# Hybrid decoder step on one core: four moves in a hand-written instruction order

## The chip, the cores and the metric

The kernel runs on one core of a Trainium2 chip. The metric is the device time of one execution in microseconds (us); the figure for a kernel is the median of its runs. A separate execution was recorded by the hardware profiler, and every time of a single instruction below comes from that one. The engines are PE (matrix multiply; PEld is its weight load, which has rows of its own), DVE (vector), ACT (scalar), POOL (GpSimd) and SP, which here only issues transfers. Each engine works through its own instructions in order, and engines wait for each other through semaphores.

## What is computed

One layer of a decoder trunk, for a prompt of 512 tokens and for 8 samples of 4 tokens, 544 columns together, model width 1024, in float32:

```python
h = RMSNorm_pre(x)
x_r, q, k, v, g = split(h @ W_in)
A = RG_LRU(conv4(x_r))                        # 8 gate blocks
B = windowed_attention(q, k, v)               # 8 heads, window 128
m = (sigmoid(g_A) * (A @ W_A) + sigmoid(g_B) * (B @ W_B)) @ W_out
x = x + RMSNorm_post(m)
u = conv3(RMSNorm_pre2(x) @ W_up)             # 2 x 4096 columns
y = x + RMSNorm_post2((gelu(u_gate) * u_val) @ W_down)
```

Beside y the kernel returns new states. Two of them matter here: the last two up-projected rows of the prompt and of each sample (`p_ffn_conv`, `s_ffn_conv`), called the state rows below.

## The kernel before

**Products.** Every float32 operand is split in two parts, high and low, and each product is three passes on PE: high by high, high by low, low by high. ACT makes the high part of a weight tile (L283, L1463) and DVE the low part by a subtraction (L290, L168, called from `wsplit_lo` and `do_low`); in the first column POOL makes it. The names in the profile carry this: `wh_`/`wl_` are the parts of a weight, `hH`/`hL`, `b11H`, `fH`/`fL` those of an activation. The 544 columns go in two halves, 256 and 288 or 272 and 272.

**Order.** The order on PE is written out by hand throughout, and on ACT and DVE in all the code that the change touches: an instruction waits behind everything that was issued earlier on its engine, whether it needs it or not. The order on POOL and SP is left to the scheduler. In the mixer a `step` is one weight column for one half, followed by a `tick`; `start_at(t, gen)` puts a generator on a list, and `sides` runs its next piece when `now` has reached its time. In the feed-forward part a `slot` follows each product: it runs what `later` and `result` have put down for this turn, then `consumed` (which splits the weights four units ahead and issues loads ten units ahead), then `round_`, a tick of 0.5.

**The start (L480 to L499).** The first two blocks of 128 tokens are turned on PE (`turn_a`, tile `ps_ta`), ACT makes `hH` (L452) and DVE `hL` (L453, in the profile L177, the helper `stt`). The first weight column comes in two transfers, one for each four k; DVE casts its high parts (L285) and POOL subtracts. The products go to `pm_first`. Then follow `pmin` products of the next columns. `xsquare` sums squares for the norm.

**Gates (L1092 to L1118).** `gate_later` is a sigmoid on ACT over 544 columns. For a column of `gl` it runs one tick after the column is done, or, where `raw` holds, at tick `SCANS[7] + c - 1`, after the square roots of the scans. Exponential, sigmoid and square root need different function tables on ACT (ACT_TABLE_LOAD). The product that needs `gl` is `lo_done` (L1131).

**Norm beside the first up tiles (L1233, L1752 to L1758).** After W_out the second half's `norm_chain` (statistics `pst_m`, factors `rep_m`, residual `x`, squares `accx`, statistics `pst_f`, factors `rep_f`, normalised `h2t`, operands `b12`, `b22`) runs in pieces, one for each slot, beside sixteen products of the first half with eight early up columns (tile `pq`, weights `wl_e`, units 1 to 16). Its piece was put down in `round_`, after the split of that slot's weight unit.

**The end (L1765 to L1945).** The plan ends with down products `pmdn` of group 6 (weights `wh_dn`), then comes the last group, QL = 7, for the second half: eight products c0 to c7 with `wh_dl`/`wl_dl`. Their results are added by DVE to `ft` (L174), squared by ACT (`sq_ft`, L1182), and added up by DVE (`acc`). Three PSUM tiles serve `pmdn` in turn, so the third product after one needs that one's `ft` addition. Three products held back (columns 5 to 7 of group 6, first half) follow, with the statistics `pst_o` between them, then the factors `rep_o`, the token-major products `ptok`, `pend`, and the output. `x1_again` brings the residual back (DMAs on SP) and turns it (`px`, `xtok`); `ffn_states` (L1733) does, twice: eight transposes into two PSUM tiles (`pfs`, `pfp`), two copies on ACT into tiles `ffn_rows_s` and `ffn_rows_p` (L1743, L1744), two DMAs on POOL's queue (L1745, L1746). These tiles, `xtok`, `x1r`, `ft`, the parts of f and of the last weights come from one pool of 53 buffers (S, L143).

Of the kernel before, what the change touches and what calls it, by code (L numbers as in the profile page):

```python
# [19 lines left out]
KD = D // P  # L20
# [58 lines left out]
GATES = (51, 53, 55, 57, 72, 73, 74, 75)  # L79
# [44 lines left out]
def hawk_step(ctx, tc, I, O):  # L124
    nc = tc.nc
    act, dve, pool, pe = nc.scalar, nc.vector, nc.gpsimd, nc.tensor
# [16 lines left out]
    def S(name, dt=F32):  # L143
        return sp.tile([P, SLOT], dt, tag="s", name=name)
# [16 lines left out]
    def f32(ap):  # L161
        return ap.bitcast(F32)

    def mm(out, l, r, start, stop):
        pe.matmul(out, l, r, start=start, stop=stop)  # L165
# [10 lines left out]
    def stt(out, a, s_, b, op0, op1):  # L176
        dve.scalar_tensor_tensor(out=out, in0=a, scalar=s_, in1=b, op0=op0, op1=op1)  # L177
# [3 lines left out]
    side, now, serial, late, last, mids, after, taps = [], [0], [0], [], [], [], [], []  # L181

    def start_at(t, gen):
        serial[0] += 1
        side.append([t, serial[0], gen])
# [62 lines left out]
    def wname(i):  # L248
        return "_".join(str(z) for z in order[i])
# [11 lines left out]
    def wclaim(target):  # L261

        target = min(target, 2 * len(order))
        for i in range(len(wraw), min(len(order), (target + 1) // 2 + 2)):
            if target:
                wload(i)
        got = list(range(wnext[0], target))
        wnext[0] = max(wnext[0], target)
        return got

    def wsplit_hi(un, eng=None):
        i, u = un // 2, un % 2
        hl = []
        for x in "hl":
            if order[i] in in_slots:
                t_ = S(f"w{x}{u}_{wname(i)}", F32R)[:, 0:512]
                t_ = t_.rearrange("p (k n) -> p k n", k=4)
            else:
                t_ = wp.tile([P, 4, P], F32R, tag="w", name=f"w{x}{u}_{wname(i)}")
            hl.append(t_)  # L280
        raw = wraw[i][:, 4 * u:4 * u + 4, :]
        if eng is None:
            act.activation(hl[0], raw, AF.Copy)  # L283
        else:
            eng.tensor_copy(hl[0], raw)  # L285
        wunits[un] = hl
        return raw, hl

    def wsplit_lo(raw, hl, eng=None):
        (eng or dve).tensor_tensor(out=hl[1], in0=raw, in1=f32(hl[0]), op=ALU.subtract)  # L290
# [53 lines left out]
    def step(key, X, a, done, target=None, look=2, quick=False):  # L344

        first_ = key == order[0] and a == 0
        ps = first_ps if first_ else PM("pm" + "_".join(str(z) for z in key) + f"_{a}")
        if first_:
            pass
        elif quick:  # L350
            mmhalf(ps, key, X, a, range(4))
            now[0] += 0.5
            sides()
            mmhalf(ps, key, X, a, range(4, 8))
            done(a, ps)
        elif len(wunits) <= 2 * FIRST and a == 0 and key in order[1:FIRST]:
            mmhalf_low_last(ps, key, X, a)
        else:
            mmhalf(ps, key, X, a)
        tick(upto(key, a, look) if target is None else target, 0.5 if quick else 1)  # L360
        if first_:
            after.append(lambda: mids.insert(1, lambda: done(a, ps)))
        elif not quick:
            (last if len(wunits) <= 2 * FIRST and a == 0 else late).append(lambda: done(a, ps))
# [39 lines left out]
    def dummy(z):  # L404
        mm(pw[:, (z % 4) * P:(z % 4 + 1) * P], ones, ones, True, True)
# [23 lines left out]
    def xsquare(i, z, on_act):  # L429
        n = TOK[i][1]  # L430
        j_, x_, o_ = T(f"jk{i}_{z}")[:n, 0:512], xt[i, z][:n, 0:512], ss[:n, z, i:i + 1]
        if on_act:
            act.activation(j_, x_, AF.Square, accum_out=o_)
        else:
            dve.scalar_tensor_tensor(out=j_, in0=x_, scalar=1.0, in1=x_, op0=ALU.mult, op1=ALU.mult, accum_out=o_)
# [14 lines left out]
    def hsplit(k, a, ps):  # L450
        g = pv[:, G_PRE + k:G_PRE + k + 1]
        act.activation(h.get(k, a, 0), ps, AF.Copy, scale=g)  # L452
        stt(h.get(k, a, 1), ps, g, f32(h.get(k, a, 0)), ALU.mult, ALU.subtract)  # L453
# [4 lines left out]
    u0, u1 = wclaim(2)  # L458
    first_ps = PM("pm_first")

    def first_mm(k, i0, i1, start=False, stop=False):
        mm(first_ps[:, :256], wunits[k // 4][i0][:, k % 4, :], h.get(k, 0, i1), start, stop)
# [3 lines left out]
    def turn_a(z):  # L466
        for k in range(4 * z, 4 * z + 4):
            if not z:
                ps_ta.append(PX(f"ps_ta{k}"))
            for q in range(2):  # L470
                pe.transpose(turned_a(k)[:, q * P:(q + 1) * P], xtile(q, k), ident)

    def turned_a(k):
        return ps_ta[k % 4][:, k // 4 * 256:k // 4 * 256 + 256]

    def first_low(z):
        for k in range(4 * z, 4 * z + 4):
            first_mm(k, 1, 0, stop=k == KD - 1)

    turn_a(0)  # L480
    for z in range(FILL):
        dummy(z)
    for k in range(KD):
        if k % 4 == 0:
            raw, hl = wsplit_hi((u0, u1)[k // 4], eng=dve)
        hsplit(k, 0, turned_a(k))
        if k % 4 == 0:
            wsplit_lo(raw, hl, eng=pool)
        first_mm(k, 0, 0, start=k == 0)
        if k == 3:  # L490
            turn_a(1)
        if k % 4:
            first_mm(k - 1, 0, 1)
        if k % 4 == 3:
            first_mm(k, 0, 1)
        if k == 3:
            first_low(0)
    first_low(1)
    xsquare(1, 1, False)  # L499

# [539 lines left out]
    def once(f, *args):  # L1040
        f(*args)
        yield
# [39 lines left out]
    def gate_done(dst, c, name, raw):  # L1082
        def f(a, ps):
            lo, hi = HALF[a]
            if a == 0:
                dst[c] = S(f"{name}{c}")
            scaled(dst[c][:, lo:hi], ps, a)
            if a == 1 and not raw:
                start_at(now[0] + 1, once(gate_later, dst, c))
        return f  # L1090
# [19 lines left out]
        for a in range(2):  # L1110
            step(("ao", c), A, a, ao_done(c), look=1 if now[0] + 1 <= GATES[3] + 2 else 2)
    for c in range(8):
        raw = 75 + 2 * c > GATES[7] + 2 and c < 7
        for a in range(2):
            step(("in", 20 + c), h, a, gate_done(gl, c, "gl", raw), look=1 if now[0] + 1 <= GATES[7] + 2 else 2)
        if raw:
            start_at(SCANS[7] + c - 1, once(gate_later, gl, c))
# [267 lines left out]
    nearly = len(units)  # L1385
# [105 lines left out]
    def consumed(k=1, lag=1, limit=10 ** 6):  # L1491
        at[0] += k
        ahead(min(at[0] + AHEAD + more[0], limit), lag)
# [24 lines left out]
    def round_(dt=0.5):  # L1518
        tick(0, dt)
# [67 lines left out]
    def result(f, *args):  # L1587
        todo.setdefault(turn[0] + 1, []).insert(0, lambda: f(*args))

    def slot(k=1, lag=1, limit=10 ** 6):  # L1590

        for f in todo.pop(turn[0], []):
            f()
        if k:
            consumed(k, lag, limit)
        turn[0] += 1
        round_()


    ec, qps = {}, {}  # L1600
# [132 lines left out]
    def ffn_states():  # L1733
        os_ = O["s_ffn_conv"].rearrange("o b i (m n) -> (o b i m) n", n=D)
        op = O["p_ffn_conv"].rearrange("o b i (m n) -> (o b i m) n", n=D)
        for kk in range(2):
            px = PX(f"pfs{kk}")
            py = PX(f"pfp{kk}")
            for j in range(4):
                pe.transpose(px[:, j * P:(j + 1) * P], sfT[:, 4 * kk + j].rearrange("p r m -> p (r m)"), ident)  # L1740
                pe.transpose(py[:16, j * P:(j + 1) * P], stage_p[:, 4 * kk + j].rearrange("p r m -> p (r m)"), ident)
            o1, o2 = S(f"ffn_rows_s{kk}"), S(f"ffn_rows_p{kk}")
            act.copy(o1[:, 0:512], px)  # L1743
            act.copy(o2[:16, 0:512], py[:16, :])  # L1744
            pool.dma_start(out=os_[:, kk * 512:(kk + 1) * 512], in_=o1[:, 0:512])  # L1745
            pool.dma_start(out=op[:, kk * 512:(kk + 1) * 512], in_=o2[:16, 0:512])  # L1746
            yield
# [4 lines left out]
    for z in range(0, len(early), 2):  # L1752
        for u in range(2):
            for j in early[z:z + 2]:
                plain("e", j, u, 0)
                slot(1, 0, nearly)
        if z == 6:
            ffn_prev()  # L1758
    at[0], s_ = nearly - AHEAD, 0
# [5 lines left out]
    for i, x in enumerate(plan):  # L1765
        more[0] = min(4, max(0, i - len(plan) + LASTS))
        if x[0] == "s":
            pair(*x[1:])
            slot()
        elif x[0] == "q":  # L1770
            plain(*x)
            slot(x[3])
        else:
            _, q, c, a = x
            down(q, c, a, down_done(q, c))
            slot(a)
        if i == len(plan) - 8:
            start_at(now[0] + 1, x1_again())
            start_at(now[0] + 5, ffn_states())

    yp, ys = O["y_p"][0], O["y_s"].rearrange("b t d -> (b t) d")
    sq7 = {}
# [194 lines left out]
```

## Time and profile before

| what | value |
|---|---|
| median of 3 runs | 997.41 us (997.02 to 998.38) |
| profiled execution, its own time | 998.21 us |
| its span, first to last instruction | 996.4 us |
| mean granted PE clock | 0.997 |
| instructions | 20123 |
| busy: ACT, POOL | 561.3 us (56%), 160.6 us (16%) |
| transfers | 135.62 MB, mean 136 GB/s |

Times in the profile run from the start of the span; 1.8 us of the execution's own time lie outside it. A group row gives line, engine, operation, output and inputs, count and busy time; a bracket gives the idle time of the engine just before and what ended it. A matmul's end is modelled and overlaps the next one's start, so gaps of PE are read from start to start or from the weight loads.

### The profile page before, as it was taken

The page shows a single profiled execution, that of the slowest core. Times are in us where ns is not written, and L with a number is a line of the kernel's source. Part 1 is how long each engine was busy: PE and PEld are TensorE (multiplying, and loading weights), DVE is VectorE, ACT ScalarE, POOL GpSimd, SP SyncE. Part 2 cuts the span into 40 slices and gives each one's busy share as a digit, 9 for nine tenths or more (in the row PEclk, how much of TensorE's full clock was granted, in tenths as well). Part 3 has the DMA queues.
Part 4 walks back from the last instruction along what each step waited for, and adds up shares of the span by engine and source line. Part 5 has one row for each costly group of instructions (what it writes and reads, how often), then busy time and mean ns, then how long its engine had stood idle before and what let it go on. Part 6 is the DMA issues. An engine that isn't in the chain of part 4 may idle for free.

```text
span 996.4 us, 20123 instructions
## 1 busy us (share of the span) xinstructions
PE 984.2 (99%) x7783; PEld 973.6 (98%) x7783; DVE 745.8 (75%) x1609; ACT 561.3 (56%) x1358; POOL 160.6 (16%) x269
## 2 busy tenths in 40 slices
PE   9999999999999999999999999999999999999997
PEld 8999999999999999999999999999999999999986
DVE  6777678766848655688877778888888888888745
ACT  6544434468367525456767665656565656565642
POOL 2062000002505341210011111111111111111004
PEclk9999999999999999999999999999999999999999
DMA  7765222333323535246058585858585858577412
GB/s 207 190 219 183 66 84 86 107 86 100 91 65 105 176 112 151 63 135 180 15 130 182 134 189 131 189 130 189 129 190 129 191 127 191 128 185 197 148 46 90
DMA packets 210999, 135.62 MB, mean 136 GB/s; under 512 B 8845, under 2 KB 197021, under 8 KB 210872
## 3 DMA queue, kind: packets, MB, share of 16 engines
q1 hardware_dynamic: 198920, 112.72, 39.9%
q0 software_dynamic: 11920, 19.59, 11.9%
q10 hardware_dynamic: 64, 2.04, 0.6%
q8 instruction: 61, 1.00, 0.4%
q14 instruction: 34, 0.28, 0.1%
HBM read 111.78 MB, written 11.37 MB: 124 GB/s over the span
## 4 chain that ended last, share of the span: by engine, by line
PE 93%; issue 4%; DVE 2%; DMA 1%; ACT 0%; POOL 0%; SPq 0%; DVEq 0%; ACTq 0%; POOLq 0%
PE pmin L165 22%; PE pmdn L165 16%; PE pux L1526 15%; PE puy L1526 8%; PE pq L1526 6%; PE pmout L165 5%; PE pmao L165 5%; PE pmlo L165 5%; PE puz L1526 4%; PE pg L165 1%; PE psc L165 1%; PE pvp L165 1%; PE ptok L165 1%; PE pt L819 1%; DMA raw_in<-in_w_in_dram 0%
## 5 line engine op out<-in xcount | busy, mean ns | idle before, releaser
L165 PE MATMUL pmin<-hH,wh_in 128*128 128x256 f32 (+1 forms) x568 | 164.6, 292 | 0.0
L165 PE MATMUL pmin<-hL,wh_in 128*128 128x256 f32 (+1 forms) x568 | 162.3, 288 | 0.0
L165 PE MATMUL pmin<-hH,wl_in 128*128 128x256 f32 (+1 forms) x568 | 159.1, 288 | 0.0
L165 PE MATMUL pmdn<-fH,wh_dn 128*128 128x256 f32 (+1 forms) x448 | 130.1, 290 | 2.3 <-DVE ft L174 2.3
L165 PE MATMUL pmdn<-fH,wl_dn 128*128 128x256 f32 (+1 forms) x448 | 129.9, 290 | 0.0
L165 PE MATMUL pmdn<-fL,wh_dn 128*128 128x256 f32 (+1 forms) x448 | 129.4, 289 | 0.0
L177 DVE SCALAR_TENSOR_TENSOR uc<-u,fv,uc 128x560 f32<-128x560 f32 x128 | 101.9, 796 | 13.3 <-ACT uc L1557 13.2
L165 PEld LDWEIGHTS pmin<-hH,wh_in 128*128 128x128 f32 x568 | 107.2, 189 | 1.4 <-issue 1.2
L165 PEld LDWEIGHTS pmin<-hL,wh_in 128*128 128x128 f32 x568 | 107.3, 189 | 0.1
L165 PEld LDWEIGHTS pmin<-hH,wl_in 128*128 128x128 f32 x568 | 104.7, 188 | 0.2 <-issue 0.2
L165 PEld LDWEIGHTS pmdn<-fH,wh_dn 128*128 128x128 f32 x448 | 85.0, 190 | 3.0 <-DVE ft L174 1.6
L165 PEld LDWEIGHTS pmdn<-fL,wh_dn 128*128 128x128 f32 x448 | 85.2, 190 | 0.0
L165 PEld LDWEIGHTS pmdn<-fH,wl_dn 128*128 128x128 f32 x448 | 85.1, 190 | 0.0
L1652 ACT COPY u<-pux 128x272 f32<-128x272 f32 x52 | 20.1, 386 | 84.4 <-PE pux L1526 84.4
L168 DVE TENSOR_TENSOR u<-puy,u 128x240 f32<-128x240 f32 (+2 forms) x78 | 24.6, 343 | 49.5 <-PE puy L1526 32.6
L283 ACT ACTIVATE wh_in<-raw_in 128x512 fp32r<-128x512 f32 x70 | 42.8, 627 | 29.1 <-issue 18.1
L174 DVE TENSOR_TENSOR ft<-ft,pmdn 128x256 f32<-128x256 f32 (+1 forms) x104 | 45.2, 434 | 16.8 <-PE pmdn L165 16.8
L290 DVE TENSOR_TENSOR wl_in<-raw_in,wh_in 128x512 fp32r<-128x512 f32 x70 | 47.9, 695 | 1.0 <-ACT wh_in L283 1.0
L1557 ACT ACTIVATE uc<-u,fv 128x560 f32<-128x560 f32 x64 | 48.3, 756 | 0.0
L1452 POOL DMA_DIRECT2D raw_up_s<-raw_up_s x26 | 22.7, 872 | 101.4 <-DMA raw_up_s<-raw_up__10513 4.5
L168 DVE TENSOR_TENSOR wl_dn<-raw_dn,wh_dn 128x512 fp32r<-128x512 f32 x56 | 38.2, 683 | 0.0
L165 PE MATMUL pmout<-mH,wh_out 128*128 128x272 f32 x128 | 37.5, 293 | 0.0
(779 smaller groups left out, 3382.6 us busy)
## 6 DMA issues: line engine op xcount, KB each, us to landing
raw_in<-in_w_in_dram SPq DMA_DIRECT2D x35, 512.0 KB
raw_dn<-in_w_down_dram SPq DMA_DIRECT2D x56, 256.0 KB
raw_up_s<-in_w_up_dram SPq DMA_DIRECT2D x25, 512.0 KB
raw_up_s<-raw_up_s POOLq DMA_DIRECT2D x26, 256.0 KB, 5.7
raw_ao<-in_w_attn_o_dram SPq DMA_DIRECT2D x8, 512.0 KB
raw_lo<-in_w_lru_o_dram SPq DMA_DIRECT2D x8, 512.0 KB
raw_out<-in_w_out_dram SPq DMA_DIRECT2D x8, 512.0 KB
xdram<-xn POOLq DMA_DIRECT2D x8, 272.0 KB, 8.3
```

Source lines behind the costliest of these rows:

```text
L165: pe.matmul(out, l, r, start=start, stop=stop)
L168: dve.tensor_tensor(out=out, in0=a, in1=b, op=ALU.subtract)
L174: dve.tensor_tensor(out=out, in0=a, in1=b, op=ALU.add)
L177: dve.scalar_tensor_tensor(out=out, in0=a, scalar=s_, in1=b, op0=op0, op1=op1)
L283: act.activation(hl[0], raw, AF.Copy)
L290: (eng or dve).tensor_tensor(out=hl[1], in0=raw, in1=f32(hl[0]), op=ALU.subtract)
L819: pe.transpose(pt[:, (2 * ch + j) * P:(2 * ch + j + 1) * P], s3[:, j, ch * P:(ch + 1) * P], ident)
L1452: pool.dma_start(out=w["p4"], in_=w["p2"], accum_op=ALU.add)
L1526: pe.matmul(ps[:, :HN], w, x, start=start and k == 0 and i == 0, stop=stop and k == 3 and i == 2, skip_group_check=True)
L1557: act.activation(yt[j][:, 0:FLATU], u[:, 0:FLATU], AF.Copy, scale=fv[:, j:j + 1])
L1652: act.copy(e[nm_], z)
```

## The change

Four moves. (1) At the start, for each group of four k: before the cast of the weight's high part, DVE now makes two `hL` in the first group and one in the second; PE takes the four `hH` products of the first group, then the second group's transposes, then the four `hL` products, then the low parts. (2) The sigmoid of `gl` column 1 goes from one tick after its column to tick 86, to the later columns' sigmoids. (3) In the sixteen early slots the pieces that are due, the norm chain's among them, are put down before the split of the slot's weight unit. (4) `ffn_states` starts at `now + 3` in place of `now + 5`, where a slot is 0.5.

```diff
-    for k in range(KD):
-        if k % 4 == 0:
-            raw, hl = wsplit_hi((u0, u1)[k // 4], eng=dve)
-        hsplit(k, 0, turned_a(k))
-        if k % 4 == 0:
-            wsplit_lo(raw, hl, eng=pool)
-        first_mm(k, 0, 0, start=k == 0)
-        if k == 3:
+    for z in range(2):
+        for k in range(4 * z, 4 * z + 4):
+            hsplit(k, 0, turned_a(k))
+            if k % 4 == 1 - z:
+                raw, hl = wsplit_hi((u0, u1)[z], eng=dve)
+                wsplit_lo(raw, hl, eng=pool)
+        for k in range(4 * z, 4 * z + 4):
+            first_mm(k, 0, 0, start=k == 0)
+            if z and k > 4:
+                first_mm(k - 1, 0, 1)
+        if z == 0:
             turn_a(1)
-        if k % 4:
-            first_mm(k - 1, 0, 1)
-        if k % 4 == 3:
-            first_mm(k, 0, 1)
-        if k == 3:
+            for k in range(4):
+                first_mm(k, 0, 1)
             first_low(0)
+    first_mm(7, 0, 1)
     first_low(1)
...
-        raw = 75 + 2 * c > GATES[7] + 2 and c < 7
+        raw = 75 + 2 * c > GATES[7] + 1 and c < 7
...
-    def slot(k=1, lag=1, limit=10 ** 6):
+    def slot(k=1, lag=1, limit=10 ** 6, chain_first=False):
...
-        if k:
+        if k and not chain_first:
             consumed(k, lag, limit)
         turn[0] += 1
         round_()
+        if k and chain_first:
+            consumed(k, lag, limit)
...
-                slot(1, 0, nearly)
+                slot(1, 0, nearly, True)
...
-            start_at(now[0] + 5, ffn_states())
+            start_at(now[0] + 3, ffn_states())
```

## The prediction

> **What bounds the kernel.** First the page: its busy times and the granted clock.
>
> ```profile
> PE 984.2 (99%) x7783; PEld 973.6 (98%) x7783; DVE 745.8 (75%) x1609; ACT 561.3 (56%) x1358; POOL 160.6 (16%) x269
> ...
> PEclk9999999999999999999999999999999999999999
> ```
>
> PE is the bound, and the change takes no product away. It can only win where PE waits or runs slowly. So next come the waits of PE's weight loads, the sharpest list of PE's gaps.
>
> ```profile
> PEld pmdn L165 <- DVE ft L174: 1.6, 1, 1.6
> PEld pm_first L165 <- ACT hH L452: 1.3, 1, 1.3
> ...
> PEld pst_o L165 <- DVE acc L174: 0.8, 1, 0.8
> PEld pst_f L165 <- DVE accx L174: 0.7, 1, 0.7
> ```
>
> Three places: the start, the second norm (`pst_f`), the end (`ft`, `pst_o`). Elsewhere PE's list shows no gap over half a microsecond but at 942 to 947. Third, the chain that ended last, at the end, and the rows of ACT and DVE there.
>
> ```profile
> 960.46 2.28 DMA out_dram<-ffn_rows_s
> ...
> 962.84 0.57 ACT ffn_rows_p L1744
> ...
> 963.43 1.28 ACT L1897
> ...
> 970.14 4.47 PE pmdn L165 x24
> ```
>
> ```profile
> 957.96 0.59 ACT L1729 COPY xtok<-px 128x512 f32<-128x512 f32 x1 [1.97 <-DMA out_dram<-ffn_rows_s]
> ...
> 962.84 0.57 ACT L1744 COPY ffn_rows_p<-pfp 16x512 f32<-16x512 f32 x1 [2.68 <-DMA out_dram<-ffn_rows_s]
> ```
>
> ```profile
> 965.29 0.46 DVE L174 TENSOR_TENSOR acc<-acc,sq_ft 128x288 f32<-128x288 f32 x1 [5.55 <-ACT sq_ft L1182]
> ```
>
> Read it downwards. ACT cannot make the last state copy, because its buffer is still read by the transfer of the one before. Behind it in ACT's order stand a table load and the squares; DVE waits 5.55 us for a square, and behind that wait stand the `ft` additions that free PE's PSUM tiles. Why a buffer is short can be counted from the code: at c4, `ft` holds 8 of the 53, `x1r` 8, the parts of f 16, those of the last weights 16. That leaves five, for four `xtok` and four state rows. The sixth comer, the last `xtok`, waits for the first state row to land (1.97 us), and the last state row for the third (2.68 us). The count fits both rows.
>
> **Move 4, the state copies four slots sooner.** PE's rows:
>
> ```profile
> 944.17 0.29 PE L165 MATMUL pmdn<-fH,wl_dn 128*128 128x288 f32 x1
> 945.27 0.37 PE L165 MATMUL pmdn<-fH,wh_dn 128*128 128x288 f32 x1 [0.81 <-DVE ft L174]
> ...
> 951.18 0.60 PE L1727 MATMUL px<-ident,x1r 128*128 128x128 f32 x4
> 951.53 0.38 PE L165 MATMUL pmdn<-fH,wh_dl 128*128 128x288 f32 x1
> ...
> 953.19 0.60 PE L1727 MATMUL px<-ident,x1r 128*128 128x128 f32 x4
> ...
> 954.42 0.38 PE L165 MATMUL pmdn<-fH,wh_dl 128*128 128x288 f32 x1
> ```
>
> `px` alone takes 0.35 us of PE (951.18 to 951.53), with the eight state transposes 1.23, so these cost 0.88. At `now + 3` the first eight fall between the last two products of group 6, the gap after 944.17: steps of 0.13 us would put the next product at 944.30, and it starts at 945.27. The 0.88 fit in that 0.97 and are no longer paid. The inputs are ready: the last row states are stored by ACT before 941. Were the gap closed by an earlier `ft`, the 0.88 would be paid again. The second eight fall behind c0 and cost what they did. First term: **0.88 us**.
>
> ```profile
> 964.54 0.29 PE L165 MATMUL pmdn<-fH,wl_dl 128*128 128x288 f32 x1
> 966.17 0.39 PE L165 MATMUL pmdn<-fH,wh_dn 128*128 128x256 f32 x1 [1.34 <-DVE ft L174]
> ...
> 967.58 0.28 PE L165 MATMUL pmdn<-fH,wl_dn 128*128 128x256 f32 x1
> 968.47 0.83 PE L165 MATMUL pst_o<-ones,acc 128*128 128x1 f32 x6 [0.62 <-DVE acc L174]
> ```
>
> Next the wait. ACT's weight parts, a copy, and the product c4:
>
> ```profile
> 944.76 3.74 ACT L1463 ACTIVATE wh_dl<-raw_dl 128x512 fp32r<-128x512 f32 x7
> ...
> 954.59 0.59 ACT L1743 COPY ffn_rows_s<-pfs 128x512 f32<-128x512 f32 x1 [0.18 <-PE pfs L1740]
> ```
>
> ```profile
> 956.90 0.38 PE L165 MATMUL pmdn<-fH,wh_dl 128*128 128x288 f32 x1
> ```
>
> The copies now run behind four of those seven parts, at 947 to 948 (two, some 0.5 us each), and about 951; buffers then: 48 held at most, plus two state rows, one `xtok`, two state rows, 53 in all, and the next `xtok`, at 952.7 at the earliest, takes a buffer whose transfer started by 948.5 and landed about 951. No wait is left. I ran ACT and DVE forward slot by slot with the durations of before. ACT's copies push the last three weight parts back by 1.0 us, to 949.5, needed at c4 (956.9). The square of c6 ends near 963.3, its addition near 963.8, the addition of c7's result at 964.6. PE would end c7 at 963.9. The first held product then finds its PSUM tile free since about 961, and `pst_o` its sums. So 964.67 to 966.17 goes, **1.50 us**, and 967.70 to 968.47, **0.77 us**. Late next would be the factors, 1.9 us after `pst_o`, beside 2.8 us of held products: not late. On POOL's queue the four DMAs move into a long idle stretch; on SP's queue nothing of this step stands, and `x1r` is not moved:
>
> ```profile
> 955.48 0.58 POOL L1745 DMA_DIRECT2D out_dram<-ffn_rows_s  x1 [28.35 <-ACT ffn_rows_s L1743]
> ```
>
> Last the clock, in stages: busy times with counts, then the granted clock.
>
> ```profile
> 4.43:7.84 3.41, 2.22 (x18) 2.02 (x17) 1.79 (x6) 1.57 (x4) 0.67 (x1) 1.00 0.90 268
> ...
> 963.47:966.88 3.41, 2.07 (x17) 1.84 (x16) 1.07 (x3) 2.51 (x5) 0.70 (x2) 1.00 0.04 10
> 966.88:970.30 3.42, 2.79 (x23) 2.50 (x22) 1.39 (x4) 1.20 (x4) 0.00 (x0) 1.00 0.00 0
> 970.30:973.71 3.41, 3.41 (x19) 3.41 (x18) 2.10 (x10) 0.14 (x1) 0.00 (x0) 0.52 0.00 0
> ```
>
> From 970.30 PE has about half its clock for 3.41 us. The stage ahead held the 0.77 us wait and 1.53 us of `pst_o`, whose one-column products do little, and so some 1.1 us of dense work; the one before that held 1.9 and was not followed by a loss. Without the waits the stage with `pst_o` keeps at least 1.9. I take the loss as gone: the 24 held products took 4.47 us, twelve in a row at full clock 1.53 (966.17 to 967.58 and a step of 0.12), so **1.41 us**. Its bounds are 0 (the clock halves all the same) and 1.7 (half of 3.41).
>
> The Trainium skill, "TensorE: Matmul & The Clock Gate", Part 1, "What's actually happening", says that PE falls to half clock after at least one idle window of about 3.4 us. By that rule neither wait here, 1.57 us at most, could have cost the clock, the loss would have another cause and stay, and the sum would be 1.4 us smaller; the trace shows the half clock after less idle than that.
>
> Sum of move 4: 0.88 + 1.50 + 0.77 + 1.41 = 4.56 us.
>
> **Move 1, the start.**
>
> ```profile
> 6.66 0.43 DVE L285 CAST wh_in<-raw_in 128x512 fp32r<-128x512 f32 x1 [1.62 <-DMA raw_in<-in_w_in_dram]
> ...
> 9.21 0.43 DVE L285 CAST wh_in<-raw_in 128x512 fp32r<-128x512 f32 x1 [0.55 <-DMA raw_in<-in_w_in_dram]
> ...
> 9.55 1.65 DVE L177 SCALAR_TENSOR_TENSOR hL<-ps_ta,pv,hH 128x256 fp32r<-128x256 f32 x4
> ```
>
> ```profile
> 11.01 1.15 ACT L283 ACTIVATE wh_in<-raw_in 128x512 fp32r<-128x512 f32 x2 [0.75 <-DMA raw_in<-in_w_in_dram]
> ```
>
> ```profile
> 11.25 0.19 PEld L165 LDWEIGHTS pm_first<-hL,wh_in 128*128 128x128 f32 x1 [0.20 <-DVE hL L177]
> 11.36 0.54 PEld L165 LDWEIGHTS pm_first<-hH,wl_in 128*128 128x128 f32 x4
> ```
>
> Both casts wait for transfers, so they stay; the lows made ahead fill DVE's idle time. The last `hL` then ends one low (0.41 us, a quarter of 1.65) earlier, near 10.87, and `pm_first` near 11.56 in place of 11.83. But the next column's first high part is ready only at 11.01 + 0.57, and some 0.1 later for PE: 11.69. The gain is **0.14 us**; bounds 0.41 (all of one low) and, if the tokens' second halves land after 7.7, where PE now wants them, a loss of as much.
>
> **Move 3, the chain ahead of the weights.**
>
> ```profile
> 436.04 0.91 DVE L177 SCALAR_TENSOR_TENSOR mt<-mt,pv,rep_m 128x272 f32<-128x272 f32 x2 [0.72 <-PE rep_m L165]
> ...
> 446.95 1.45 DVE L174 TENSOR_TENSOR accx<-accx,sq_x 128x272 f32<-128x272 f32 x3
> ```
>
> DVE has no idle time between these two, and the 0.65 us of PE before `pst_f` hang on the second. Between them stand five weight lows (units 8 to 12, 0.6 us each). In the new order they are units 7 to 11: unit 7, which ran ahead of 436.04 while DVE would have waited for `rep_m`, now waits behind it, and unit 12 falls behind the sums. Five lows either way, so `accx` ends when it did. Behind the waiting `mt` now stand those lows; units 10 and 11 come late by about 0.5 us for PE, but what PE loses there it waits less at `pst_f`. **Cost 0**; bounds a gain of 0.65 (the wait gone) and a loss of 0.5 (the late lows not covered). Buffers of these weights come free up to 3 us later; the loads into them feed products from 452 on, and the early columns before them hide that; if not, the bound of 0.5 grows by their delay.
>
> **Move 2, the sigmoid.** It spares two table loads of 1.28 us on ACT near 300 and adds one sigmoid near 324, in idle time:
>
> ```profile
> 326.28 0.63 ACT L1018 ACTIVATE lH<-hs 128x512 fp32r<-128x512 f32 x1 [2.78 <-DVE hs L1013]
> ```
>
> PE has no gap from 280 to 360: **0**; if ACT's burst there ran over, the loss would be at most one sigmoid, shorter than a table load.
>
> **The number.** 4.56 + 0.14 = 4.70 us. The profiled execution would go from 998.21 to 993.5, its span from 996.4 to 991.7. The median of the runs lies 0.80 us lower than that execution and the terms are the same: 997.41 - 4.70 = **992.7 us**. Its own range, with moves 1 and 3 inside their bounds, is 992.3 to 993.4.
>
> **Rivals.**
> - *The clock halves anyway*, at `pst_o` or near 947, where new transposes stand beside two short waits: 992.7 + 1.4 = **994.1**. For it: 1.53 us of one-column products stay. Against it: the stage 4.43 to 7.84, mostly transposes and a wait, was followed by full clock. The Trainium skill, the same page, Part 4, says transposes do not count as PE-busy in the same way; by that rule the stage after 946.9 would be thin and could halve, giving this rival's time.
> - *Move 3 shortens the chain*: 992.7 - 0.65 = **992.05**. Against it: DVE without idle time.
> - *The wait stays*: buffers come free in another order than I counted, and ACT waits 2.7 us for a landing again, now elsewhere in the end. Only 0.88 and 0.14 remain: **996.4**.
> - *Slower*: the early copies stand in ACT's order ahead of three weight parts of the last group. If they wait there for buffers, the first 4.8 us are covered (parts ready about 952 with DVE's lows, needed at 956.9), each further microsecond is PE's loss. It turns slower from 4.8 + 4.7 = 9.5 us, beyond three landings in series at 0.59 + 2.28 each; four, 11.5 us, give 992.7 + 6.7 = **999.4**. Against it: the count.
>
> **Chances.** Forecast 0.67, clock 0.14, chain 0.09, wait stays 0.06, slower 0.04. The range 991.8 to 994.8 holds the first three, 0.90, less some for unknown spreads. About 0.2%, 2.0 us, is what a measurement tells from no change: faster by more than that 0.90, within it 0.06, slower 0.04.
>
> **What would show it.** In the new profile: `pfs` at about 944.3 and 949.5; no ACT wait on `ffn_rows`; no gap ahead of the first held product and of `pst_o`; clock 1.00 to the end; the 24 products in 3.1 us; `pst_f` still waiting 0.1 to 0.7; first `pmin` near 11.7. A wait of ACT on a state row's landing, or a half clock after `pst_o`, would make the number wrong.

## The result, and the profile after

| what | before | after |
|---|---|---|
| median of 6 runs, us | 998.09 (997.02 to 998.4) | 993.17 (993.09 to 993.23) |
| ratio, 95% interval | | 0.9953 [0.994, 0.9965] |
| profiled execution: its own time, its span, us | 998.21, 996.4 | 993.09, 991.3 |
| mean granted clock of that execution | 0.997 | 0.999 |
| first held product, `pst_o`, `rep_o` start at, us | 966.17, 968.47, 974.45 | 963.76, 965.18, 969.36 |

The change is faster, by 0.5%: 992.7 was forecast, 993.17 came, inside the range. The runs of before do not agree as well as those of after: among the 67 that were timed beside the experiments, those with a mean clock of 0.999 take 996.25 to 997.70 us (median 996.83) and those with less 997.69 and more, which the sections behind this one come back to.

The page of after: the share of the chain of work in which nothing that the profile shows was waited for ("issue") was 4% before, with 2% on DVE and 1% on a DMA.

```profile
span 991.3 us, 20127 instructions
...
PE 982.1 (99%) x7783; PEld 972.3 (98%) x7783; DVE 747.2 (75%) x1609; ACT 558.9 (56%) x1356; POOL 160.2 (16%) x269
...
PE 96%; DVE 1%; ACT 1%; issue 0%; POOL 0%; DVEq 0%; ACTq 0%; POOLq 0%
```

From c0, at 947.45, to the last product the chain now runs on PE alone. The waits of PE's weight loads, the same view as before:

```profile
PEld pm_first L165 <- ACT hH L452: 1.2, 1, 1.2
...
PEld pq L1527 <- DVE wl_e L168: 0.6, 1, 0.6
...
PEld pmdn L165 <- ACT ffn_rows_s L1746: 0.6, 1, 0.6
```

The 1.6 us ahead of the held product and the 0.8 us ahead of `pst_o` are gone. The 0.7 us ahead of `pst_f` are gone too, but 0.6 us stand ahead of a `pq` in their place. Next, ACT at the end of after (start, duration, then in brackets the idle time before and what ended it):

```profile
944.73 2.18 ACT L1464 ACTIVATE wh_dl<-raw_dl 128x512 fp32r<-128x512 f32 x4
946.81 0.56 ACT L1746 COPY ffn_rows_s<-pfs 128x512 f32<-128x512 f32 x1
947.27 0.57 ACT L1747 COPY ffn_rows_p<-pfp 16x512 f32<-16x512 f32 x1
947.75 1.67 ACT L1464 ACTIVATE wh_dl<-raw_dl 128x512 fp32r<-128x512 f32 x3
...
951.01 0.57 ACT L1747 COPY ffn_rows_p<-pfp 16x512 f32<-16x512 f32 x1
...
952.72 0.59 ACT L1732 COPY xtok<-px 128x512 f32<-128x512 f32 x1 [0.80 <-ACT acc L1178]
```

No bracket names a transfer any more: the four state copies have their buffers, the weight parts end near 949.4, and no copy behind them waits for one either. What PE does with it:

```profile
944.26 0.27 PE L1743 MATMUL pfs<-ident,sfT 128*128 128x128 f32 x1
...
945.24 0.38 PE L165 MATMUL pmdn<-fH,wh_dn 128*128 128x288 f32 x1
```

```profile
963.76 0.28 PE L165 MATMUL pmdn<-fH,wh_dn 128*128 128x256 f32 x1
...
965.18 0.72 PE L165 MATMUL pst_o<-ones,acc 128*128 128x1 f32 x6
965.76 0.81 PE L165 MATMUL pst_o<-ones,sq 128*128 128x1 f32 x6
966.43 0.36 PE L165 MATMUL pmdn<-fH,wh_dn 128*128 128x256 f32 x1
...
969.36 0.65 PE L165 MATMUL rep_o<-dg_o,ones 128*128 128x288 f32 x2
```

The first eight state transposes start at 944.26, and the product behind them at 945.24, where it started before (945.27) without them: they cost nothing. At the end the rows follow each other without a bracket, and the 24 held products take 2.93 us (966.43 to 969.36). The granted clock there, by stages (length, then the busy time and count of PE, PEld, DVE, ACT and POOL, then the clock):

```profile
964.96:968.37 3.41, 3.41 (x32) 3.41 (x31) 1.32 (x9) 0.26 (x1) 0.00 (x0) 1.00 0.00 0
968.37:971.79 3.42, 3.42 (x21) 2.96 (x20) 2.44 (x8) 0.00 (x0) 1.14 (x2) 1.00 0.00 0
```

PE is busy throughout and the clock stays at 1.00. From the start of `rep_o` in both profiles the gain by then is 974.45 - 969.36 = 5.09 us.

### The profile page after: what moved, and what is told of

Read it like the earlier page. It is cut to its first block, busy times and chain, and to the rows that moved or that the text cites. A ratio compares the mean times of both kernels' runs of the same rounds, so it can differ in the third digit from the quotient of the medians.

```text
span 991.3 us, 20127 instructions
## 1 busy us (share of the span) xinstructions
PE 982.1 (99%) x7783; PEld 972.3 (98%) x7783; DVE 747.2 (75%) x1609; ACT 558.9 (56%) x1356; POOL 160.2 (16%) x269
## 4 chain that ended last, share of the span: by engine, by line
PE 96%; DVE 1%; ACT 1%; issue 0%; POOL 0%; DVEq 0%; ACTq 0%; POOLq 0%
PE pmin L165 22%; PE pmdn L165 17%; PE pux L1527 16%; PE puy L1527 8%; PE pq L1527 6%; PE pmout L165 5%; PE pmao L165 5%; PE pmlo L165 5%; PE puz L1527 4%; PE pg L165 1%; PE psc L165 1%; PE pvp L165 1%; PE ptok L165 1%; PE pt L820 1%; PE ps_warm L165 0%; PE ps_tb L526 0%
```

## The experiments

Theory: the gain is move 4's alone, because ACT no longer waits for a buffer, and with the waits the half clock goes. Rivals: the other moves share in the gain; the order of the copies and not the buffers; a clock that falls for another reason.

### The four moves apart

Before, with move 4 alone:

```diff
-            start_at(now[0] + 5, ffn_states())
+            start_at(now[0] + 3, ffn_states())
```

> The kernel before with move 4 alone (state copies four slots sooner). My theory, that the gain is move 4's: 4.6 us less than before by the terms of the prediction, 4.9 by what the new profile shows, so 993.2 to 993.6 and within 0.3 us of the changed kernel. Rival, that the moves at the start and in the norm carry part of it: 994 or more. In its profile: no ACT wait on a state row's landing, no half clock ahead of the output.

After, with move 4 undone:

```diff
-            start_at(now[0] + 3, ffn_states())
+            start_at(now[0] + 5, ffn_states())
```

> The changed kernel with move 4 undone (moves 1, 2 and 3 alone). My theory: within 0.3 us of before, since the three together gave 0.03 to 0.07 us in the profile up to 942 us; the end waits and the half clock of before are back. Rival, that they carry part of the gain: 1 us or more faster.

Move 4 alone gave 993.16 us (992.82 to 993.24), ratio 0.9955 [0.9942, 0.9968]; the other three gave 997.33 (996.7 to 998.53), ratio 0.9997 [0.9988, 1.0006]. So move 4 gives the gain of all four (993.17), and the other three together change nothing that can be measured; the interval reaches about 0.9 us either way. The second run brought something that the forecast did not know. Its profiled execution (996.88 us) has both waits of before, and no half clock behind them:

```profile
965.40:968.80 3.40, 1.77 (x13) 1.57 (x13) 2.23 (x6) 1.48 (x4) 0.00 (x0) 1.00 0.00 0
968.80:972.20 3.40, 3.39 (x28) 3.31 (x29) 1.57 (x10) 0.70 (x2) 0.00 (x0) 1.00 0.00 0
```

```profile
966.43 0.39 PE L165 MATMUL pmdn<-fH,wh_dn 128*128 128x256 f32 x1 [1.33 <-DVE ft L174]
968.73 0.83 PE L165 MATMUL pst_o<-ones,acc 128*128 128x1 f32 x6 [0.60 <-DVE acc L174]
```

The same waits and the same statistics, and the clock stays at 1.00. Of the twelve executions seven took 996.7 to 997.34 us at a mean clock of 0.999, five 998.11 to 998.53 at 0.997 or 0.998. Nothing lies between 997.34 and 998.11, so here, by time and mean clock together, some executions pay for a half clock and others do not. The mean clock alone does not tell it: executions of after read 0.998 to 1.000 and agree within 0.14 us.

### Is it the buffers?

Before, with the copies at their old place, and the state rows from another pool of buffers than the 53:

```diff
-            o1, o2 = S(f"ffn_rows_s{kk}"), S(f"ffn_rows_p{kk}")
+            o1, o2 = T(f"ffn_rows_s{kk}"), T(f"ffn_rows_p{kk}")
```

> The kernel before, nothing moved, but the four state-row tiles taken from the pool T (10 buffers) in place of the pool S (53 buffers). My theory, that ACT waits for a buffer of S: the ACT waits of 1.97 and 2.68 us go, with them the two PE waits and the half clock, 1.5 + 0.77 + 1.41 = 3.7 us and 0.3 for the statistics that then run without a restart, so 994.1 to 994.4; the 0.88 us for the first eight transposes stay, since they are not moved into the gap. Rival, that it is the place of the copies in ACT's order and not the buffer: 0 to 0.5 us faster than before.

993.9 us (993.78 to 994.19), ratio 0.9964 [0.9951, 0.9976]: without any move, other buffers alone give most of the gain, so the shortage of buffers made the waits. What is missing to 993.17, 0.73, is the first term of the forecast, the transposes in the gap, worked out there as 0.88.

Then before, with the copies only two slots sooner:

```diff
-            start_at(now[0] + 5, ffn_states())
+            start_at(now[0] + 4, ffn_states())
```

> The kernel before with the state copies two slots sooner (now + 4), half the way of move 4. My count of the 53 buffers: first state rows behind the first residual tile (51), two more residual tiles (53), then the second state rows take the buffers of the first, long landed, and only the last residual tile waits under 1 us for a landing, which ACT's slack covers. So both PE waits go and the clock's loss, and only the 0.88 us of transposes in PE's gap are missed: 994.0. Rival, that each slot sooner buys its share: half of 4.7 us, 995.5.

996.29 us (995.03 to 997.07), ratio 0.9977 [0.9967, 0.9987], above both expected times: the count behind the expectation named the copy that would wait, but put its wait under 1 us. Six executions at a mean clock of 0.999 have a median of 995.47, six at 0.997 or 0.998 one of 996.76: the half clock comes and goes here too. The profiled execution (996.63) is of the second kind; ACT first, then PE:

```profile
955.73 0.59 ACT L1743 COPY ffn_rows_s<-pfs 128x512 f32<-128x512 f32 x1 [0.22 <-PE pfs L1740]
...
960.47 0.59 ACT L1729 COPY xtok<-px 128x512 f32<-128x512 f32 x1 [3.34 <-DMA out_dram<-ffn_rows_s]
```

```profile
966.92 0.83 PE L165 MATMUL pst_o<-ones,acc 128*128 128x1 f32 x6 [0.50 <-DVE acc L174]
967.76 0.83 PE L165 MATMUL pst_o<-ones,sq 128*128 128x1 f32 x6
```

The last state row finds a buffer, and it is now the last `xtok` that waits for a transfer, 3.34 us. The count of the forecast gives the place: behind the first two state rows and three `xtok` the 53 are out, and the next copies take buffers only as transfers land. ACT has time for most of the wait: the held product no longer waits, but `pst_o` still does, and the transposes do not reach the gap. Two slots thus buy about the 1.50 us of the first wait: at a mean clock of 0.999 on both sides the six executions of before timed beside this run have a median of 997.12, and 997.12 - 995.47 = 1.65. The next two slots buy the rest.

### What halves the clock

After, with twelve more products of one column (not used) behind `pst_o`:

```diff
+        thin = PX("thin")
+        for i in range(12):
+            mm(thin[:, i:i + 1], acc[:, i % 3 * P:(i % 3 + 1) * P], ones[:, 0:1], True, True)
```

> The changed kernel with twelve more one-column products behind the statistics at the end, into a tile that nobody reads; PE gets no wait, only thin work. My theory, that thin work counts as little as a wait for the clock: the products' own time, 2.5 us by the 1.25 us that six such products take now, and in most executions half clock for 3.41 us behind them, 1.4 us more: 997 us, and runs about 1.4 us apart where the window's place differs. Rival, the rule of the Trainium skill (TensorE: Matmul & The Clock Gate, Part 1) that it takes an idle window of about 3.4 us: 2.5 us alone, 995.7, at full clock throughout.

997.56 us (997.35 to 998.87), ratio 1.0004 [0.9995, 1.0012]. The products take 2.67 us (the next starts at 969.13), so 993.17 + 2.67 = 995.84 without a loss of clock; 1.7 us more were measured by the median, 1.55 in the profiled execution (997.39). Four of the twelve, 998.69 to 998.87 at a mean clock of 0.995 or 0.996, lost about 1.4 us more than that; none of these has a profile.

```profile
966.46 2.82 PE L165 MATMUL thin<-ones,acc 128*128 128x1 f32 x24
```

```profile
965.40:968.80 3.40, 3.40 (x32) 3.40 (x32) 1.69 (x9) 0.26 (x1) 0.00 (x0) 1.00 0.00 0
968.80:972.20 3.40, 3.40 (x21) 3.40 (x21) 0.42 (x1) 0.00 (x0) 0.00 (x0) 0.63 0.00 0
972.20:975.60 3.40, 3.40 (x19) 3.02 (x18) 1.33 (x4) 0.00 (x0) 0.73 (x1) 0.87 0.02 5
```

PE is busy for the whole of the first stage, 3.40 of 3.40 us, and the clock falls all the same, for about 3.4 us that overlap the next two. All twelve executions have a mean clock of 0.995 to 0.998, and the fastest of them lies 1.5 us above 995.84. No idle time is needed: one-column products alone halve the clock here. The Trainium skill, "TensorE: Matmul & The Clock Gate", Part 1, "What's actually happening", has the clock fall after an idle window of about 3.4 us; the length of the half clock agrees with it, the condition as its words stand does not.

Two more runs at the same place ask what does count. After, with thirty transposes (not used), and after, with eleven products of 512 columns (not used):

```diff
+        for i in range(30):
+            pe.transpose(thin[:, i % 4 * P:(i % 4 + 1) * P], acc[:, i % 2 * P:(i % 2 + 1) * P], ident)
```

> The kernel after, with thirty more 128x128 transposes (not used) behind the statistics pst_o, where the earlier run had twelve one-column products in 2.67 us. At 0.09 to 0.11 us each they take 2.6 to 3.3. Theory (what halved the clock there was work of one column, not idle time; transposes do little more, but the stage 4.43 to 7.84 of before held them at full clock): no half clock, 993.17 plus the time of the transposes, 995.8 to 996.5. Rival (transposes do not count as work of PE for the clock, so they act as the thin products did): a half clock window behind them and some 1.5 us more, 997.3 to 998.

```diff
+        for i in range(11):
+            mm(thin, F.t[QL * CH][0][:, 0:P], usplit["dl", 0, 0][0].rearrange("p k n -> p (k n)"), True, True)
```

> The kernel after, with eleven more products of 512 columns (not used) at the same place, some 0.24 us each, so 2.6 us of dense work. Both theories: full clock, 993.17 + 2.6 = 995.8. If the clock halves here too, neither thinness nor transposes were the cause, but only that the end became longer.

With transposes 996.53 us (996.06 to 996.68), ratio 0.9982 [0.9973, 0.9991]; with dense products 995.86 (995.72 to 996.19), ratio 0.9981 [0.9972, 0.999]. The transposes of the first:

```profile
966.43 3.47 PE L1794 MATMUL thin<-ident,acc 128*128 128x128 f32 x30
```

```profile
965.40:968.80 3.40, 3.40 (x33) 3.40 (x33) 1.69 (x9) 0.26 (x1) 0.00 (x0) 1.00 0.00 0
968.80:972.20 3.40, 3.40 (x32) 3.40 (x30) 0.42 (x1) 0.00 (x0) 0.00 (x0) 1.00 0.02 5
```

The held products start again at 969.65, so the transposes take 3.22 us, and 993.17 + 3.22 = 996.39, close to what came; the dense ones take 2.66 us, 993.17 + 2.66 = 995.83. All eleven executions of each stay at a mean clock of 0.998 or more, and none lies over 0.4 us above its median, so none paid for a half clock. Transposes of 128 columns, 0.107 us each, hold the clock up; one-column products, 0.111 us each, do not. The Trainium skill, the same page, Part 4, has transposes not counting as busy in the same way; here they count.

The traces say more, since they hold the moments at which the granted clock changes. In each of the 13 profiles these lie whole multiples of 3.413 us apart: in before at 4.47, 970.44, 973.85 and 994.33, with 283, 1 and 6 of them between. Where the first one falls differs from one execution to the next (4.47 in before, 6.43 with moves 1 to 3), and so each execution has its own row of windows of 3.413 us. Cut along these windows, before and the kernel with moves 1 to 3:

```profile
967.03:970.44 3.41, 2.78 (x22) 2.50 (x22) 1.24 (x4) 1.19 (x4) 0.00 (x0) 1.00 0.00 0
970.44:973.85 3.41, 3.41 (x19) 3.41 (x17) 2.10 (x10) 0.00 (x1) 0.00 (x0) 0.50 0.00 0
```

```profile
965.57:968.99 3.42, 1.96 (x15) 1.76 (x15) 2.40 (x6) 1.36 (x3) 0.00 (x0) 1.00 0.00 0
968.99:972.40 3.41, 3.40 (x30) 3.31 (x30) 1.58 (x10) 0.70 (x2) 0.00 (x0) 1.00 0.00 0
```

The window with the more busy PE, 2.78 us, is the one that was followed by half clock: all 1.53 us of `pst_o` lie in it, and what is left, without the restart behind `pst_o`, is about 1.0 us of wider products. The other window holds 1.96, but only 0.26 of `pst_o`, and so some 1.4 us of wider products. Counted like this from the start times, an estimate, every window up to the last product with 1.1 us or less (before, twelve more products, two slots sooner) was followed by half clock, and none with 1.5 or more in any of the 13 profiles; near 1.4 both were seen. In after the window with the least holds 2.1, and since `pst_o` takes 1.25 us there, no placing of the windows would bring it below 2.

### Can the waits that are left be closed?

Two waits of some 0.6 us are left in after, in the norm and ahead of c0. DVE makes weight lows ahead of both. After, with two lows (units 10 and 11 of the early ones) on POOL in place of DVE:

```diff
-        sub(hl[1], src, f32(hl[0]))
+        if key in units[9:11]:
+            pool.tensor_tensor(out=hl[1], in0=src, in1=f32(hl[0]), op=ALU.subtract)
+        else:
+            sub(hl[1], src, f32(hl[0]))
```

> The changed kernel with the low parts of units 10 and 11 in the early slots on POOL in place of DVE (1.28 us each there, at the start). My theory, that the norm chain is bound by DVE and that five weight lows stand in it in either order: with two fewer the sums end 1.2 us sooner, the PE wait of 0.6 us at units 10 and 11 goes and none comes back at the statistics: 0.6 us less than the changed kernel, 992.6. Rival, that the chain is paced by POOL's additions and the matmuls between them: the wait moves back to the statistics, 993.2; or POOL's two lows delay its additions: slower than that.

The same for two lows of the last group (`key in (("dl", 0, 0), ("dl", 1, 0))`), and for both together:

> The changed kernel with the first two low parts of the last weight group on POOL in place of DVE. PE still waits 0.56 us before the last group for a result addition that stands behind those two lows on DVE. Theory: that wait goes, 0.5 us less than the changed kernel, 992.7. Rival: the wait hangs on ACT's weight parts, as the row's releaser says; then nothing changes, 993.2.

> The two edits before this one together on the changed kernel. Theory: the gains add, 1.1 us, 992.1. Rival: less, where one wait hides behind the other; they are 500 us apart, so I expect none of that.

All three missed the gain that the theory promised. In the norm 994.49 us (994.14 to 996.03), ratio 0.9963 [0.9949, 0.9977]; at the end 993.23 (993.15 to 993.41), ratio 0.9947 [0.9931, 0.9963]; both 994.62 (994.15 to 995.96), ratio 0.996 [0.9948, 0.9972]. In the run with the norm's lows alone one sees POOL's rows, ACT's behind them, and the waits of PE:

```profile
443.40 1.29 POOL L1470 TENSOR_TENSOR wl_e<-raw_up__5714,wh_e 128x512 fp32r<-128x512 f32 x1 [1.12 <-ACT wh_e L1464]
444.65 0.98 POOL L1261 TENSOR_TENSOR x<-x,mt 128x272 f32<-128x272 f32 x1
446.69 1.40 POOL L1470 TENSOR_TENSOR wl_e<-raw_up__5712,wh_e 128x512 fp32r<-128x512 f32 x1 [1.06 <-ACT wh_e L1464]
```

```profile
445.67 0.43 ACT L1267 ACTIVATE sq_x<-x 128x272 f32<-128x272 f32 x1 [2.07 <-POOL x L1261]
446.00 0.61 ACT L1464 ACTIVATE wh_e<-raw_up__5712 128x512 fp32r<-128x512 f32 x1
```

```profile
PEld pq L1530 <- POOL wl_e L1470: 1.0, 1, 1.0
...
PEld pst_f L165 <- DVE accx L174: 0.6, 1, 0.6
```

A low takes 1.3 to 1.4 us on POOL and 0.6 on DVE. The first one holds up POOL's own addition `x`, ACT waits 2.07 us for it (0.90 in after), and behind that wait stands the high part that the second low needs. So PE waits 1.0 and 0.6 us where it waited 0.6, which is 1.0 of the 1.3 us lost; the rival, that POOL's lows delay its own additions, holds. With both pairs moved, the profiled execution (995.88) lost the clock in the norm too: it stood at 0.50 from 450.46 to 453.87, behind a window with two waits, the one-column products of `pst_f` and some 1.4 us of wider ones. At the end there is another cause, seen in DVE's rows beside POOL's:

```profile
942.40 1.49 DVE L177 SCALAR_TENSOR_TENSOR uc<-u,fv,uc 128x560 f32<-128x560 f32 x1
...
946.36 0.46 DVE L174 TENSOR_TENSOR ft<-ft,pmdn 128x288 f32<-128x288 f32 x1
946.72 2.04 DVE L168 TENSOR_TENSOR wl_dl<-raw_dl,wh_dl 128x512 fp32r<-128x512 f32 x2
```

```profile
941.98 1.32 POOL L1470 TENSOR_TENSOR wl_dl<-raw_dl,wh_dl 128x512 fp32r<-128x512 f32 x1 [14.87 <-ACT wh_dl L1464]
946.13 1.48 POOL L1470 TENSOR_TENSOR wl_dl<-raw_dl,wh_dl 128x512 fp32r<-128x512 f32 x1 [2.84 <-ACT wh_dl L1464]
```

The same `uc` takes 0.80 us in after (at 942.38), and two such lows 1.29. While POOL subtracts, DVE's operations with two inputs in SBUF hardly get on: `uc` ends at 943.89, 0.59 behind POOL's end at 943.30, and the two lows at 948.76, 1.15 behind 947.61, so that 0.9 us beside POOL were worth some 0.2 us of work or less each time. The addition to `ft`, with one input in PSUM, takes its usual 0.46. So f is 0.7 us late and PE waits 0.9 us for it ahead of group 6's last product. The wait ahead of c0 is gone for it, and nothing is won. The Trainium skill, "SBUF — State Buffer", "Who interferes with whom", says that DVE and GpSimd share one pair of ports as an exclusive lock; the trace agrees, with the numbers above.

The other way is to put work into the gap ahead of c0. After, with the second state's transposes one slot behind the first's in place of two, between the last product of group 6 and c0:

```diff
             pool.dma_start(out=op[:, kk * 512:(kk + 1) * 512], in_=o2[:16, 0:512])
-            yield
+            yield 0.5
```

> The kernel after, with the second state's eight transposes, copies and transfers one slot behind the first's in place of two: they then stand between the last product of group 6 and c0, where PE waits 0.56 us from 946.85. Theory (the transposes cost what no gap covers, and the 53 buffers still suffice): 0.56 of their 0.88 us lie in the gap, so 993.17 - 0.56 = 992.6, the gap after 946.85 gone, c0 about 0.3 later. Rival (the earlier copies delay the last weight parts or a buffer is short again): 993.2 or more, with a wait of PE on a weight part at c1 to c4, or of ACT on a transfer.

992.53 us (992.26 to 992.68), ratio 0.9947 [0.9934, 0.9959], the fastest of all, some 0.64 under after.

```profile
946.98 0.28 PE L1743 MATMUL pfs<-ident,sfT 128*128 128x128 f32 x1
...
947.77 0.38 PE L165 MATMUL pmdn<-fH,wh_dl 128*128 128x288 f32 x1
```

c0 starts 0.32 us later than in after (947.45), c1 at 949.79 in place of 950.35, and that 0.56 lasts to `rep_o` (968.80). The buffers still suffice: no copy waits for a transfer.

## Why the prediction was right, point by point

| step of the forecast | forecast, us | profile | 
|---|---|---|
| first eight transposes in the gap | 0.88 | 0.91, c7 at 962.17 in place of 963.08, with 0.03 from ahead of it |
| wait ahead of the first held product | 1.50 | 1.50, from the two rows' 2.41 less 0.91 |
| wait ahead of `pst_o` | 0.77 | 0.88, from 3.29 less 2.41 |
| `pst_o` itself | 0 | 0.28, from 1.53 to 1.25 |
| half clock over the 24 products | 1.41 | 1.52, from 4.45 (970.00 to 974.45) to 2.93 |
| move 1, the start | 0.14 | 0.07, first `pmin` weights at 11.76 in place of 11.83 |
| moves 2 and 3 | 0 | 0: with move 1, all that lies ahead of 945 is 0.03 earlier |

**Move 4** went as reckoned: the buffers, the gap, and the wait that was a chain of copies, squares and sums. The transposes, the order of ACT and the time of the next `xtok` (952.7 forecast, 952.72 measured) came where the forecast had put them. The statistics were mis-sized. They come in two sets of six, and before, the second set waited as well:

```profile
968.47 0.83 PE L165 MATMUL pst_o<-ones,acc 128*128 128x1 f32 x6 [0.62 <-DVE acc L174]
969.31 0.83 PE L165 MATMUL pst_o<-ones,sq 128*128 128x1 f32 x6
```

```profile
968.82 0.44 ACT L1177 ACTIVATE sq<-ft 128x288 f32<-128x288 f32 x1 [0.89 <-DVE ft L174]
```

The square of c7 ended at 969.26, and its six products started at 969.31, 0.84 behind the first six; in after they follow by 0.58. Most of the 0.28 is this gap; it carries no bracket and was taken for PE's own time. The 0.11 more in the row of the wait ahead of `pst_o` lies in the twelve held products in front of it, 1.53 us behind a wait and 1.42 without one.

**The clock** was right for the profiled execution and mis-sized as a term of the median. The step that does not hold is the one that says of the median that "the terms are the same". It subtracted 1.41 us from the middle one of three runs, 997.41, which by its time did not hold them (their clocks are not on record; at 0.999 the 67 reach 997.70). Over the three sets of before that were timed beside the experiments, 23 of 67 executions have a mean clock of 0.999, with a median of 996.83 us. Thirteen others, 999.37 to 1001.67 us at 0.994 or 0.995, lost more than one half clock window costs; none of them has a profile, and where they lost the rest stays open. Without the clock's term the rows of the table up to `pst_o` sum to 0.91 + 1.50 + 0.88 + 0.28 = 3.57 (the little that move 1 leaves is in the first of them), and 996.83 - 3.57 = 993.26, near after's 993.17; the profiled execution, 998.21, comes to 993.12 with 1.52 more. So three errors lie in the forecast of the median: 1.41 us taken off for a clock term that the 997.41 did not hold; the other way, 0.28 too little off for the rest (3.29 against 3.57); and 997.41 itself, 0.58 above the 996.83 of such executions. That they leave only 0.47 us between 992.7 and 993.17 is in part luck. For the profiled execution the forecast took 0.39 us too little (4.70 against 5.09), most of it `pst_o`.

**Why the waits cost the clock at all** was argued from the dense work in a stage, 1.1 us in the stage ahead of the loss and 1.9 in the one before it, and the traces bear that out: about 1.0 and 1.8 in the windows of 3.413 us, 2.1 in after. What the argument left out is that the windows lie elsewhere in each execution. By the rows of the kernel with moves 1 to 3, which ran at full clock, a window that begins between 966.5 and 968.3 would hold less than 1.4 us of wider products; that is 1.9 of 3.41 us of possible beginnings, an estimate of 55%, where 5 of its 12 executions and, by the mean clock, 44 of 67 of before paid. In after no beginning does it. This is read from 13 traces that agree; no run set the place of the windows on purpose.

**Move 3** did what the forecast said. DVE made five lows between the same two points, the sums `accx` start at 446.91 in place of 446.95, and PE waits 0.62 us for a late low up to 445.6 in place of 0.65 for the sums up to 448.5. The rival of a shorter chain had 0.09 and is out. **Move 1** gave half its estimate: in after the second cast started at 9.47 us, behind a low that waited for ACT, and the last `hL` ended at 11.06, not at 10.87. With first products of that execution 0.36 us later than in before (7.57 against 7.21), little more can be read from one profile. The rivals of the wait that stays and of the slower kernel are out by the rows of ACT in after; that they could have come true is shown by the copies two slots sooner, where a wait of 3.34 us moved to another copy.

## What to carry to other kernels

When an engine waits for a transfer that only writes results out, count the buffers of the pool at that moment, by name: the count says which copy will be late, and whether a few slots sooner or another pool of buffers cures it. Before a term of the clock goes into a forecast, look at several executions, since one profile shows a loss that is paid in some of them only; where one-column products stand beside waits, count the wider products in any 3.4 us: with some 1 us of them there was such a loss, with 2 there was none. And put work that depends on nothing into the gaps that stay: eight transposes cost nothing in one, 0.88 us a slot later.

## What the runs showed of the hardware

- PE's clock halves for about 3.4 us behind 2.7 us of one-column products and 1.25 us of `pst_o`, without any idle time of PE, in twelve of twelve executions by their times; behind 3.2 us of transposes or 2.7 us of products of 512 columns at the same place it stays at full speed, in eleven of eleven each. One such half clock cost 1.5 us in the profiles of before and of the kernel with twelve more products.
- In all 13 profiles the changes of the granted clock lie whole multiples of 3.413 us apart, and the first lies elsewhere in each. A window of that length with 1.1 us or less of products wider than one column was followed by half clock each time, one with 1.5 or more never.
- With 2.4 us of waits beside the statistics it therefore comes in part of the executions: judged by a mean clock below 0.999, in 44 of 67 of before and in 5 of 12 of the kernel with moves 1 to 3 alone.
- A subtraction of POOL over 512 columns holds up DVE's operations with two inputs in SBUF until it ends (0.80 us became 1.49), and leaves one with an input in PSUM alone (0.46). Subtractions moved to an idle POOL were not off DVE's path here.
